# A pad of 160 bytes behind a small table, and where the tiles behind it lie

## The chip, the cores and the metric

One core of a Trainium2 chip runs the whole kernel in one launch. The metric is the device time of one execution in microseconds, given as the median of several runs. A measurement of a change against this kernel can tell about 0.2%, some 3 us, from no change.

## The reference, cut to what matters

One encoder layer on 256 tokens of 2048 features, in float32:

```python
proj = rms_norm(x, attn_norm) @ w_in            # columns: qa ka va qb kb vb ga gb
ya = windowed_gqa(qa, ka, va, ...)              # 8 query heads, 1024 wide
yb = dilated_attention(qb, kb, vb, ...)         # merged over 3 groups, 512 wide
merged = sigmoid(ga) * (ya @ w_branch_a) + sigmoid(gb) * (yb @ w_branch_b)
x = x + merged @ w_out
hf = rms_norm(x, ffn_norm)
g = dwconv_centred(hf @ w_ffn_gate, conv_w, conv_b)      # 5632 wide
x = x + (gelu(g) * (hf @ w_ffn_up)) @ w_ffn_down
x = x + sigmoid(rms_norm(x, ple_norm) @ w_ple_gate) * (p @ w_ple_proj)
return rms_norm(x, final_norm)
```

Nearly all of the work is in the products with weight matrices; the weights are read once, 277 MB in all.

## The kernel before, in words

**Pairs.** A float32 number is kept as two parts, a high one and a low one, both in the fast matmul type. A weight block is 128 x 128. Weights come from memory in pieces of 16 blocks (`raw`, line 174); ACT rounds a run of 8 blocks to `whi` (line 190), DVE subtracts to get `wlo` (line 191). An activation tile holds for each block of 128 features 512 columns: 256 tokens' high parts and 256 low parts, 2048 bytes per partition. `block` (lines 195 to 206) issues two matmuls for each weight block, here called a pair: line 201 holds `whi` and streams all 512 columns, line 202 holds `wlo` and streams the 256 high columns. The held tile is the stationary operand, the streamed one the moving operand. Each matmul has a weight load of its own, which overlaps the matmul before it.

**Moving operands.** `product` (line 207) runs the pairs of one 128-wide slice of outputs, 16 of them for an input of 2048. The streamed tile is given by `movers` (line 662): `hs`, `merged`, `hf`, all named `mov` and taken from the pool `big`; `yab` (line 337), the outputs of the two mixers, 8 and 4 blocks; and `act` (line 682), the gelu half, 22 blocks. `wide_product` (line 214) works the other way round: it holds a slice of the activations and streams the weights, three matmuls for each (lines 224 to 226); the value projections and the last stage use it.

**Order.** `_plan` (line 62) lists the products. First queries, keys and values; then a round for each of 16 slices: the gates `ga` and `gb` (16 pairs each) and, two rounds later, the branch products `ba` (8 pairs from `yab`) and `bb` (4 pairs from `yab`); then the output projection `o`; then for each half of the MLP gate and up products by turns (16 pairs each, 44 products) and 16 down products `d0` or `d1` (22 pairs each from `act`); then the embedding products. The loop at line 672 issues them in this order, and TensorE runs them in order. Attention's small matmuls are put between pairs at fixed places by `run_due` (line 330): scores (lines 430 to 432 and 449), transposes (line 484), values (lines 430 to 432 and 499). The row norms come in the same way: sums (line 285), then a spread over the partitions (line 308), whose moving operand is `rdg` (line 300). In `d1`, `flip` (line 633) puts four transposes after every second product.

**Places in on-chip memory.** Pools are laid one behind the other in the order in which they are opened: constants, `wpool` (`raw`, `whi`, `wlo`), `big` (`mov`), `sc` (small tiles, `tot` first and `tb` behind it), then `att` (`yab`, attention's tiles), whose place `ff` (`act` and the MLP's tiles) takes later. A tile's size is rounded up to 32 bytes per partition. In the built program `raw`, `whi`, `wlo` and every `mov` start at residue 160 modulo 512 bytes; so does `tb`. `tb` takes 80 bytes, rounded to 96. `yab` and `act` both start at 154112, residue 0.

Of the kernel before, what the change touches and what calls it, by code (L numbers as in the profile page):

```python
# [10 lines left out]
F32 = mybir.dt.float32  # L11
# [16 lines left out]
NH = QH + BH  # L28
NBUCK = 32
# [104 lines left out]
def _encoder(ctx: ExitStack, tc, xt, pt, cols, table, onehot, mask, ident_in, last_gain, wts, out):  # L134
# [110 lines left out]
    sc = ctx.enter_context(tc.tile_pool(name="sc", bufs=2))  # L245
# [95 lines left out]
    hba = hb[:, :QH * AW].rearrange("p (h c) -> p h c", c=AW)  # L341
    hbb = hb[:, QH * AW:].rearrange("p (h c) -> p h c", c=BW)
    oh = ap_.tile([NBUCK, 2 * T], F32, name="oh", tag="near", bufs=1)
    tb = sc.tile([NBUCK, NH], F32, name="tb", bufs=1)
    mk = ap_.tile([NH, 2 * T], F32, name="mk", tag="s1", bufs=2)

    order = [(0, 1), (0, 0, 1), (0, 1, 3), (0, 3, 7), (1, 2), (0, 7, 11), (0, 11, PIECE), (2, 3)]
# [440 lines left out]
```

## Time and profile before

| | |
|---|---|
| median of three runs | 1501.67 us (1501.54 to 1502.61) |
| the profiled execution, its own time | 1501.95 us |
| its span | 1500.1 us |
| TensorE busy | 99% of the span |
| VectorE, ScalarE busy | 70%, 51% |
| memory read | 277 MB, 186 GB/s over the span |
| granted TensorE clock | 0.998 |

The span runs from the first to the last instruction that the profiler shows; the time of the execution has 1.85 us around it. A line of the profile names the source line, the engine, the operation, the tile written and the tiles read, in the order moving, then stationary for a matmul. Matmuls overlap: the record of one runs on after the next has begun, so durations do not add up to the time. The time from one start to the next does.

### The profile page before, as it was taken

How to read it: one execution, taken by the hardware profiler on the slowest of the kernel's cores; microseconds unless marked ns; L12 is line 12 of the kernel's file. 1: busy time of each engine (PE TensorE's matmuls, PEld its weight loads, DVE VectorE, ACT ScalarE, POOL GpSimd, SP SyncE). 2: the span in 40 equal slices, each digit the busy share in tenths (PEclk: the TensorE clock that was granted, in tenths of full speed). 3: DMA queues.
4: the chain of work that ended last, by engine and by line, in shares of the span. 5: the costliest groups of instructions: out<-in, count | busy, mean ns of one | idle time of the engine just before them, and what ended most of it. 6: DMA issues, size and time to landing. Idle time of an engine off the chain costs nothing.

```text
span 1500.1 us, 21525 instructions
## 1 busy us (share of the span) xinstructions
PE 1483.0 (99%) x8392; PEld 1292.5 (86%) x8392; DVE 1045.0 (70%) x1631; ACT 767.0 (51%) x1175; POOL 4.6 (0%) x9
## 2 busy tenths in 40 slices
PE   9999999999999999999999999999999999999996
PEld 8888888888888888888888888888888888888885
DVE  7685764666676776778888885557888887656564
ACT  7564544445555555555555554444555555555553
POOL 0000000000000000000000000000000000000000
PEclk9999999999999999999999999999999999999999
DMA  8744344445555555555555555554555555554552
GB/s 316 254 156 182 137 168 172 169 169 188 181 193 196 182 184 204 177 216 194 182 188 194 196 184 183 195 190 180 192 197 191 182 190 196 177 189 172 193 196 84
DMA packets 45233, 280.92 MB, mean 187 GB/s; under 512 B 4996, under 2 KB 9860, under 8 KB 12876
## 3 DMA queue, kind: packets, MB, share of 16 engines
q1 hardware_dynamic: 44268, 277.31, 51.7%
q10 hardware_dynamic: 864, 2.24, 0.4%
q8 instruction: 66, 1.08, 0.3%
q14 instruction: 35, 0.29, 0.1%
HBM read 277.39 MB, written 2.14 MB: 186 GB/s over the span
## 4 chain that ended last, share of the span: by engine, by line
PE 96%; DVE 2%; DMA 1%; ACT 1%; issue 0%; POOL 0%; SPq 0%; DVEq 0%; POOLq 0%; ACTq 0%
PE acc L201 53%; PE acc L202 27%; PE acc L224 4%; PE acc L226 4%; PE acc L225 4%; PE first L201 1%; PE first L202 1%; DVE wlo L191 1%; DMA raw<-in_wts 1%; PE pt L484 0%; PE misc L633 0%; DMA x<-in_xt 0%; PE misc L499 0%; PE sp L449 0%; ACT whi L190 0%
## 5 line engine op out<-in xcount | busy, mean ns | idle before, releaser
L191 DVE TENSOR_TENSOR wlo<-raw,whi 128x1024 fp32r<-128x1024 f32 (+1 forms) x519 | 632.0, 1218 | 407.4 <-ACT whi L190 407.1
L201 PE MATMUL acc<-mov,whi 128*128 128x512 f32 x2608 | 911.4, 394 | 1.5 <-DVE v L539 1.5
L190 ACT ACTIVATE whi<-raw 128x1024 fp32r<-128x1024 f32 (+1 forms) x519 | 547.6, 1055 | 645.0 <-PE acc L201 394.0
L202 PE MATMUL acc<-mov,wlo 128*128 128x256 f32 x2608 | 728.2, 279 | 0.0
L201 PEld LDWEIGHTS acc<-mov,whi 128*128 128x128 f32 x2608 | 488.6, 187 | 112.0 <-DVE v L539 1.7
L202 PEld LDWEIGHTS acc<-mov,wlo 128*128 128x128 f32 x2608 | 491.9, 189 | 0.2
L201 PE MATMUL acc<-act,whi 128*128 128x512 f32 x704 | 247.5, 394 | 0.0
L202 PE MATMUL acc<-act,wlo 128*128 128x256 f32 x704 | 196.5, 279 | 0.0
L201 PEld LDWEIGHTS acc<-act,whi 128*128 128x128 f32 x704 | 131.9, 187 | 31.1
L202 PEld LDWEIGHTS acc<-act,wlo 128*128 128x128 f32 x704 | 132.0, 187 | 0.0
L224 PE MATMUL acc<-whi,mov 128*128 128x512 f32 (+1 forms) x256 | 96.9, 379 | 0.0
L226 PE MATMUL acc<-whi,mov 128*128 128x512 f32 (+1 forms) x256 | 96.6, 377 | 0.0
L225 PE MATMUL acc<-wlo,mov 128*128 128x512 f32 (+1 forms) x256 | 96.6, 377 | 0.0
L252 ACT ACTIVATE t<-acc 128x256 f32<-128x256 f32 x227 | 83.1, 370 | 23.2 <-PE acc L202 23.2
L256 DVE TENSOR_TENSOR u<-acc,t 128x256 f32<-128x256 f32 x196 | 81.3, 418 | 2.4 <-ACT t L252 2.4
L201 PE MATMUL acc<-yab,whi 128*128 128x512 f32 x192 | 68.4, 395 | 0.0
L224 PEld LDWEIGHTS acc<-whi,mov 128*128 128x128 f32 x256 | 48.6, 190 | 9.3 <-DVE wlo L191 0.8
L226 PEld LDWEIGHTS acc<-whi,mov 128*128 128x128 f32 x256 | 48.6, 190 | 8.8
L225 PEld LDWEIGHTS acc<-wlo,mov 128*128 128x128 f32 x256 | 48.6, 190 | 8.6
L202 PE MATMUL acc<-yab,wlo 128*128 128x256 f32 x192 | 53.8, 280 | 0.0
L201 PEld LDWEIGHTS acc<-yab,whi 128*128 128x128 f32 x192 | 36.0, 188 | 8.8
L201 PE MATMUL first<-mov,whi 128*128 128x512 f32 x112 | 39.0, 400 | 0.8 <-DVE mov L269 0.8
(137 smaller groups left out, 856.5 us busy)
## 6 DMA issues: line engine op xcount, KB each, us to landing
raw<-in_wts SPq DMA_DIRECT2D x251, 1024.0 KB, 4.8
raw<-in_wts SPq DMA_DIRECT2D x12, 512.0 KB, 6.9
x<-in_xt SPq DMA_DIRECT2D x13, 128.0 KB, 6.0
mov<-hold SPq DMA_DIRECT2D x3, 514.0 KB, 6.4
mov<-hold SPq DMA_DIRECT2D x2, 768.0 KB, 7.1
mov<-in_last_gain ACTq DMA_DIRECT2D x1, 1024.0 KB, 4.8
out<-mov SPq DMA_DIRECT2D x2, 384.0 KB, 2.5
out<-mov ACTq DMA_DIRECT2D x2, 384.0 KB
```

The lines of the kernel that those rows point to most:

```text
L190: nc.scalar.activation(hi, src, AF.Copy)
L191: nc.vector.tensor_tensor(lo, src, hi.bitcast(F32), op=ALU.subtract)
L201: nc.tensor.matmul(acc, hi[:, o, :], m, start=first, stop=False, skip_group_check=True)
L202: nc.tensor.matmul(acc[:, T:], lo[:, o, :], m[:, :T], start=False, stop=last, skip_group_check=True)
L224: nc.tensor.matmul(acc, xh, hi, start=(k == 0), stop=False)
L225: nc.tensor.matmul(acc, xh, lo, start=False, stop=False)
L226: nc.tensor.matmul(acc, xl, hi, start=False, stop=(k == n - 1))
L252: keep(nc.scalar.activation(t, acc[:, T:], AF.Copy, scale=scale))
L256: nc.vector.tensor_tensor(u, acc[:, :T], t, op=ALU.add)
```

## The change

The table tile gets 40 more columns, which nothing writes or reads; the kernel uses the first 20 as before.

```diff
     oh = ap_.tile([NBUCK, 2 * T], F32, name="oh", tag="near", bufs=1)
-    tb = sc.tile([NBUCK, NH], F32, name="tb", bufs=1)
+    tb = sc.tile([NBUCK, NH + 40], F32, name="tb", bufs=1)[:, :NH]
     mk = ap_.tile([NH, 2 * T], F32, name="mk", tag="s1", bufs=2)
```

`tb` then takes 240 bytes, rounded to 256, so every tile behind it moves up by 160 bytes: the rest of `sc`, `yab` and `act` (to 154272, residue 160), and all of attention's and the MLP's tiles. The tiles ahead of it stay. On every engine the instructions and their order are the same in both programs.

## The prediction

> **What bounds the kernel now.** I read the page first (shares, chain), then a table of stretches that holds only the L201 matmuls, then the timeline where a stretch begins.
>
> ```profile
> span 1500.1 us, 21525 instructions
> PE 1483.0 (99%) x8392; PEld 1292.5 (86%) x8392; DVE 1045.0 (70%) x1631; ACT 767.0 (51%) x1175; POOL 4.6 (0%) x9
> PE 96%; DVE 2%; DMA 1%; ACT 1%; issue 0%; POOL 0%; SPq 0%; DVEq 0%; POOLq 0%; ACTq 0%
> ```
>
> TensorE is busy 99% of the span and holds 96% of the chain that ended last. Nothing else can be late enough to matter, so this change is worth what it does to the time from one matmul to the next. The page's duration of a matmul does not show that: matmuls overlap in the records.
>
> ```profile
> L201 PE MATMUL acc<-mov,whi 128*128 128x512 f32 x2608 | 911.4, 394 | 1.5 <-DVE v L539 1.5
> L201 PE MATMUL acc<-act,whi 128*128 128x512 f32 x704 | 247.5, 394 | 0.0
> L201 PE MATMUL acc<-yab,whi 128*128 128x512 f32 x192 | 68.4, 395 | 0.0
> ```
>
> By these rows mov, act and yab cost the same (394, 394, 395 ns). So I take the pitch instead: the length of a stretch in which TensorE never idles, divided by the pairs (one L201 and one L202 matmul) that start in it. The view: stretch in us from the span's start, its length, busy time of the L201 matmuls, and their count, which takes in one or two that run over an edge.
>
> ```profile
> 169.52:177.65 8.13, 8.13 (x25) 1.00 0.31 123
> 191.27:214.50 23.23, 23.23 (x68) 1.00 0.51 182
> 288.63:311.86 23.23, 23.23 (x69) 1.00 0.49 181
> 326.06:346.91 20.85, 20.85 (x61) 1.00 0.53 184
> 346.91:559.02 212.11, 212.11 (x610) 1.00 0.53 189
> 351.47:362.22 10.75, 10.75 (x33) 1.00 0.53 193
> 565.17:649.62 84.45, 84.45 (x239) 1.00 0.54 190
> 661.70:894.66 232.96, 232.96 (x674) 1.00 0.54 192
> 894.66:1017.86 123.20, 123.20 (x353) 1.00 0.53 189
> 1017.86:1261.93 244.07, 244.07 (x706) 1.00 0.53 190
> 1261.93:1388.67 126.74, 124.25 (x353) 1.00 0.50 183
> ```
>
> There are three beats, all at a granted clock of 1.00. **Middle:** the first half's down products (894.66 on), 16 products of 22 blocks, 352 pairs: 123.20/352 = 350.0 ns. Their moving operand is act. **Fast:** the gate and up products (661.70 on), 42 products of 16, 672 pairs: 232.96/672 = 346.7 ns; the second half's, 704 pairs: 244.07/704 = 346.7. **Slow:** the output projection (565.17 on), 239 pairs: 84.45/239 = 353.3; the first gate products of the mixers (326.06 on), 59 pairs: 20.85/59 = 353.4. Fast and slow stretches read the same kind of tile, mov, with the same two shapes. In the addresses that the built program gives its tiles, raw, whi, wlo and all mov tiles lie at residue 160 modulo 512 bytes, and yab and act at 0; each block is a multiple of 512 bytes, so the residue holds for every block.
>
> So residue 0 gives one beat, 350.0, and residue 160 gives two, 3.3 ns either side of it. Which one holds is not set by address: it is kept until something interrupts the stream, for 672 pairs in one row and 239 in the other. What starts each beat can be read too:
>
> ```profile
> 169.07 0.50 PE L201 MATMUL acc<-mov,whi 128*128 128x512 f32 x1 [1.52 <-DVE v L539]
> 564.23 0.87 PE L201 MATMUL acc<-mov,whi 128*128 128x512 f32 x2
> 658.84 0.59 PE L308 MATMUL misc<-rdg,ones 128*128 128x256 f32 x2
> 324.81 1.06 PE L499 MATMUL misc<-far,vf 128*128 128x128 f32 x8
> 64.87:66.95 2.08, 2.08 (x7) 1.00 0.99 377
> 659.62:661.70 2.08, 2.08 (x8) 1.00 0.47 110
> ```
>
> A stream that resumes from a wait is slow: after 169.07 (23 pairs in 8.13 us, 353.5) and after 564.23, where the second matmul starts late. After the spread of the row norms (L308) it was fast both times (the last two rows: six pairs in 2.08 us, 346.7). After a far head's last small matmuls (L499) it was fast twice (67 pairs in 23.23 us from 191.27 and from 288.63) and slow in the last case, from 326.06. And when the stream comes back from yab it is fast: from 351.47, 31 pairs in 10.75 us, 346.8; the whole mixers' row, 608 pairs at 348.9, says that the other rounds are alike. The residue 0 of yab thus resets the beat for the mixers today, and act resets it for the second half.
>
> **The change part by part.** It makes tb 160 bytes longer per partition. No instruction is added, removed or moved on any engine, and no wait; the DMA into tb writes the same 20 columns. Every tile allocated behind tb moves up by 160 bytes; x, raw, whi, wlo, mov and tot, in front of it, stay. yab and act come to residue 160, so all L201/L202 pairs are then of the kind with two beats. The sum is made against the profiled execution's 1501.95 us (span 1500.1 and 1.85 around it), 0.28 above the median of 1501.67.
>
> Step 1, first half's down products: 352 pairs from 350.0 to 346.7, -1.2 us. If slow, +1.2.
>
> Step 2, second half's: also 352 pairs, but eight groups of four transposes (L633) interrupt them. If all stay fast, -1.2 us, and the halting pairs after a reset go:
>
> ```profile
> 1262.28 0.39 PE L201 MATMUL acc<-act,whi 128*128 128x512 f32 x1
> 1262.63 0.42 PE L201 MATMUL acc<-act,whi 128*128 128x512 f32 x1
> 1263.02 0.39 PE L201 MATMUL acc<-act,whi 128*128 128x512 f32 x1
> 321.63:323.75 2.12, 2.12 (x8) 1.00 0.58 243
> 77.94:80.37 2.43, 2.43 (x8) 1.00 0.71 297
> 85.36:87.78 2.42, 2.42 (x8) 1.00 0.29 122
> ```
>
> The pair at 1262.63 takes 390 ns, 40 too many, and such a pair comes after some of the transposes too: about -0.2 us. The last three rows say how transposes leave a stream of residue 160: after eight of them slow (six pairs in 2.12 us, 353), after four fast (seven in 2.43 and in 2.42, 347 and 346). The flips are of four, but with other operands, so I take most of the products as fast: -0.8 us, bounds -1.4 and +1.2.
>
> Step 3, the mixers, 346.91 to 559.02: 13 rounds of 44 pairs and 36 at the end, 608 pairs in 212.11 us. All fast would be 608 x 346.7 ns = 210.8, -1.3 us; all slow 608 x 353.3 = 214.8, +2.7. Nothing interrupts them now except yab itself, and that reset goes with the change. So one draw, made at 324.81, decides 667 pairs together with the 59 before, which are slow now: fast there is another -0.4. I take fast: -1.7 us.
>
> Step 4, the output projection: it starts with the wait at 564.23, which stays because the last merged block is late by the same work on ACT and DVE. Slow as now: 0, with -1.6 (239 x 6.7 ns) as the other bound.
>
> Step 5, gate and up products, 1376 pairs from 661.70 on. Their beat is drawn once, at 658.84, and act no longer redraws it at 1017.86. The operands of that interruption stay where they are, except rdg, which moves with the change. Kept fast: 0. Slow: 1376 x 6.7 = +9.2 us.
>
> Step 6, attention's small matmuls (s, qf, kf, near, v): their own time is a few us in all, but they redraw the beat of the pairs between 64 and 326 us. I take 0, bounds -1 and +2. The DVE and ACT operations on moved tiles lie beside a busy TensorE; were that cover gone, they could be late only at the four or five waits already there.
>
> Step 7, the 48 matmuls of the embedding product with pw, which moves from residue 0 to 160 and is held while whi streams:
>
> ```profile
> 1396.11:1398.45 2.34, 2.34 (x12) 1.00 0.00 0
> 1401.74:1437.00 35.26, 35.26 (x157) 1.00 0.52 182
> ```
>
> Ten starts in 2.34 us with pw, 234 ns, against 155 in 35.26 with mov, 227: 48 x 7 ns = -0.3 us.
>
> Sum: -1.2 - 0.8 - 1.7 + 0 + 0 + 0 - 0.3 = -4.0 us; 1501.95 - 4.0 = 1497.95, which I round to **1498.0**.
>
> **The rivals.**
>
> *One slow draw in the mixers.* At 324.81 the stream comes out slow, as it does in the trace of before, and now no yab resets it. Price: +2.7 in place of -1.7, so the sum is -1.2 - 0.8 + 2.7 - 0.3 = +0.4 us, 1502.4. For it: that very draw is slow now, and two of the four alike were. Against it: the operands of L499 move, so the draw is made anew.
>
> *The lock turns against the long stage.* This is the slower side. If the stream leaves the L308 spread at 658.84 slow, then 1376 gate and up pairs and 352 down pairs stay slow up to the flips: +9.2 + 1.2, with the second half's down products near 0 and the mixers at -1.7 or +2.7: 1501.95 + 10.4 - 2.0 = 1510.4 or 1514.8. It decides from about half of these pairs slow. Against it: both spreads of the trace, 595 us apart and with different work ahead of them, ended fast, so that interruption seems to set the beat by itself. For it: rdg, its moving operand, shifts from residue 448 to 96, and slow beats are otherwise as common after interruptions as fast ones.
>
> *The residue is not the cause.* If act and yab run at 350.0 because of their place elsewhere (another distance to the weights, another block count), nothing but draws changes: 1501.7, within a microsecond or two. Against it: yab and act have different block counts (8, 4 and 22) and the same beat. The Trainium skill speaks for this rival: "SBUF — State Buffer", section "Who interferes with whom", gives TensorE two independent SBUF read ports, one for the moving operand and one for the weights, and says that TensorE never waits on anyone; by that rule no address could change a pitch and the time would stay. The 346.7, 350.0 and 353.3 ns above do not look like that.
>
> **How the numbers follow.** Chances: forecast 0.45, slow mixers 0.24, slow long stage 0.23, residue not the cause 0.08. The forecast's own range is 1495.5 to 1500.5 by the bounds of steps 2, 4 and 6; slow mixers 1501 to 1505; slow long stage 1507 to 1517. To hold eight in ten the range has to take in the first two and the near part of the third: 1495.5 to 1510.5. A measurement of this kernel tells about 0.2%, 3 us, from no change, so faster means under 1498.7: most of the forecast, 0.37. Slower means over 1504.7: the long stage and a little of the slow mixers, 0.27. The rest, 0.36, is within.
>
> **What would show it.** In the changed profile the down products should take 346.7 ns a pair over 352 pairs (122.0 us in place of 123.20), and no 390 ns pair should follow their start. The mixers should take 210.8 us from the first a-product to the output projection. The page's durations should stay at 394. The forecast is wrong if act still runs at 350.0, if one of the three long stretches shows 353.3, or if a new wait appears on TensorE.

## The result, and the profile after

The change makes the kernel slower: 1516.56 us in the median of four runs (1510.56 to 1517.9) against 1501.69 (1501.54 to 1502.61), ratio 1.0088 with a 95% interval of 1.0069 to 1.0106. The forecast was 1498.0, with a range from 1495.5 to 1510.5. The profiled execution took 1517.9 us, its span is 1516.1.

From the page of the changed kernel: span, chain by engine, and two groups of L201.

```profile
span 1516.1 us, 21525 instructions
PE 98%; DVE 1%; ACT 0%; DMA 0%; issue 0%; DVEq 0%; POOLq 0%; POOL 0%; ACTq 0%
L201 PE MATMUL acc<-mov,whi 128*128 128x512 f32 x2608 | 925.0, 399 | 1.5 <-DVE v L539 1.5
L201 PE MATMUL acc<-act,whi 128*128 128x512 f32 x704 | 248.9, 398 | 0.0
```

The count of instructions is the same, and TensorE holds the chain as before. No new wait stands in these rows, and yet the mov group has 13.6 us more busy time (925.0 against 911.4). The mean record is longer by 4 or 5 ns in both groups.

The table of stretches of the changed kernel, cut where the stages begin. Columns: stretch, length, busy time of L201 and their count, granted clock, DMA share, GB/s. The rows are attention, mixers, output projection, the first gate product with the row norms, gate and up of the first half, its down products, gate and up of the second half, its down products.

```profile
60.12:349.61 289.49, 189.13 (x529) 1.00 0.47 172
349.61:564.44 214.83, 214.83 (x610) 1.00 0.51 187
564.44:655.08 90.64, 90.57 (x258) 1.00 0.51 188
655.08:667.19 12.11, 11.39 (x33) 1.00 0.61 224
667.19:904.63 237.44, 237.44 (x673) 1.00 0.52 189
904.63:1029.02 124.39, 124.39 (x354) 1.00 0.51 186
1029.02:1277.75 248.73, 248.73 (x705) 1.00 0.51 186
1277.75:1404.66 126.91, 124.45 (x353) 1.00 0.51 182
```

The stages of before that the prediction did not show, attention, projection and row norms:

```profile
58.94:346.91 287.97, 187.48 (x529) 1.00 0.48 173
559.02:649.62 90.60, 90.53 (x257) 1.00 0.53 189
649.62:661.70 12.08, 11.36 (x34) 1.00 0.61 225
```

Divided by their pairs, the long rows of after are all at the slow beat: mixers 214.83/608 = 353.3 ns, gate and up 237.44/672 = 353.3 and 248.73/704 = 353.3, first down products 124.39/352 = 353.4. Not one is at 350.0 any more. The middle beat of residue 0 is gone, as the mechanism said, and what took its place is the wrong one of the two.

| stage | before | after | difference, us |
|---|---|---|---|
| up to attention | 58.94 | 60.12 | +1.18 |
| attention | 287.97 | 289.49 | +1.52 |
| mixers | 212.11 | 214.83 | +2.72 |
| projection, row norms | 102.68 | 102.75 | +0.07 |
| gate and up, both halves | 477.03 | 486.17 | +9.14 |
| down, first half | 123.20 | 124.39 | +1.19 |
| down, second half | 126.74 | 126.91 | +0.17 |
| embedding stage and end | 111.43 | 111.44 | +0.01 |
| span | 1500.1 | 1516.1 | +16.0 |

The beat of the long stage is taken in the timeline of the changed kernel at the spread of the row norms: start, duration, engine, line, tiles.

```profile
664.29 0.59 PE L308 MATMUL misc<-rdg,ones 128*128 128x256 f32 x2
...
665.07 0.40 PE L201 MATMUL acc<-mov,whi 128*128 128x512 f32 x1
...
665.43 0.40 PE L201 MATMUL acc<-mov,whi 128*128 128x512 f32 x1
...
665.78 0.40 PE L201 MATMUL acc<-mov,whi 128*128 128x512 f32 x1
```

The pairs behind L308 start at 665.07, 665.43, 665.78: 360 and 350 ns, the slow pattern. It then holds through the next three rows of the table above, 1728 pairs, and into the second half's down products up to the first flip.

### The profile page after: what moved, and what is told of

It reads as the page before. It is cut to its first block, busy times and chain, and to the rows that moved or that the text cites. A ratio compares the mean times of both kernels' runs of the same rounds, so it can differ in the third digit from the quotient of the medians.

```text
span 1516.1 us, 21525 instructions
## 1 busy us (share of the span) xinstructions
PE 1499.0 (99%) x8392; PEld 1297.5 (86%) x8392; DVE 1045.8 (69%) x1631; ACT 767.1 (51%) x1175; POOL 4.7 (0%) x9
## 4 chain that ended last, share of the span: by engine, by line
PE 98%; DVE 1%; ACT 0%; DMA 0%; issue 0%; DVEq 0%; POOLq 0%; POOL 0%; ACTq 0%
PE acc L201 54%; PE acc L202 27%; PE acc L224 4%; PE acc L226 4%; PE acc L225 4%; PE first L201 2%; PE first L202 1%; PE pt L484 0%; DMA x<-in_xt 0%; PE misc L633 0%; PE misc L499 0%; PE sp L449 0%; PE misc L430 0%; PE sp L430 0%; PE sp L432 0%; PE misc L432 0%
## 5 line engine op out<-in xcount | busy, mean ns | idle before, releaser
L201 PE MATMUL acc<-mov,whi 128*128 128x512 f32 x2608 | 925.0, 399 | 1.5 <-DVE v L539 1.5
L201 PEld LDWEIGHTS acc<-mov,whi 128*128 128x128 f32 x2608 | 490.0, 188 | 122.0 <-DVE v L539 1.7
L201 PE MATMUL acc<-act,whi 128*128 128x512 f32 x704 | 248.9, 398 | 0.0
L201 PEld LDWEIGHTS acc<-act,whi 128*128 128x128 f32 x704 | 132.2, 188 | 32.0
L201 PE MATMUL acc<-yab,whi 128*128 128x512 f32 x192 | 68.5, 399 | 0.0
L201 PEld LDWEIGHTS acc<-yab,whi 128*128 128x128 f32 x192 | 36.1, 188 | 9.0
L201 PE MATMUL first<-mov,whi 128*128 128x512 f32 x112 | 40.3, 409 | 1.2 <-DVE mov L269 1.2
```

The source lines that it names most:

```text
L201: nc.tensor.matmul(acc, hi[:, o, :], m, start=first, stop=False, skip_group_check=True)
```

## The experiments

Theory A is that of the prediction: the distance between the places of the moving and the stationary operand decides which beats there are; equal residues have two, one of them is taken at each interruption and kept, and a tile at residue 0 resets it. (`raw`, `whi` and `wlo` lie at 160 in every program here, so for the pairs a distance and a place of the moving tile alone are not told apart.) The rivals are that the moved small tiles or attention's tiles did it, or that residue 160 in act is bad by itself.

### The pad behind sc: rdg back at its place

```diff
-    yab = ap_.tile([P, QH + HG, 2 * T], FR, name="yab", bufs=1)
+    yab = ap_.tile([P, (QH + HG) * 2 * T + 40], ...)[:, 40:]      # and act in the same way
```

`tb` is as before; yab, act and attention lie where the change put them.

> The 160 bytes sit at the front of yab and of act instead of in tb: yab, act and all tiles behind them are where the change put them, but the small tiles of sc, rdg with them, are back at their old places. Theory A (the two beats of residue 160 are drawn at each interruption, and nothing resets them once yab and act lie at 160 too): the down products are fast or slow, never 350.0 ns; the mixers are one beat all through. If the place of rdg is what turned the L308 spread to the slow beat, the gate and up stage is fast again and the time some 10 us below the changed kernel, near 1506; if only the phase in which the stream reaches the spread decides, it can be slow here too, 1510 to 1517, and the runs differ among themselves. Rival B (act and yab at 160 do nothing, the moved small tiles of sc are the cause): 1501.7 and down products at 350.0.

1505.26 us in the median of ten (1498.9 to 1506.91), ratio 1.0015 (1.0002 to 1.0028). Mixers, first gate and up, first down:

```profile
349.03:563.86 214.83, 214.83 (x609) 1.00 0.53 187
666.59:899.54 232.95, 232.95 (x673) 1.00 0.54 192
899.54:1021.57 122.03, 122.03 (x353) 1.00 0.54 190
```

The long stage is fast, and now the down products run at 122.03/352 = 346.7 ns: the gain of step 1, in full. The mixers are slow as in the changed kernel. Of the ten times two are at 1498.9 and eight at 1505 to 1507; the two groups are further apart than the mixers alone can make (4.1 us), and the faster one was not profiled. One and the same program thus comes out in two groups of times; that the beat is what differs between them is not shown.

### Only rdg moved

```diff
-        dg = sc.tile([P, T], F32, name="rdg", bufs=1)
+        dg = sc.tile([P, T + 128], F32, name="rdg", bufs=1)[:, 40:40 + T]
```

The other tiles behind it move by multiples of 512 bytes, so they keep their residues. `sq` has one buffer in place of two here and in yab_only below, to make room. That alone does nothing to the long stage, which takes 232.96 us in yab_only.

> Everything as before the change but one tile: rdg, the moving operand of the L308 spread, lies at residue 96, as in the changed kernel, in place of 448. (sq gets one buffer in place of two to make room.) Theory A2 (the place of rdg decides with which beat the stream leaves the spread): the first half's gate and up products, 672 pairs, are at 353.3 ns, +4.5 us; yab and act at residue 0 still reset the mixers and the second half, which stay as before; 1505 to 1507. Rival (the slow beat of the changed kernel came with the slow mixers and projection ahead of it, not from rdg): 346.7 ns and 1501.7.

1506.8 us (1505.96 to 1508.0), ratio 1.0030 (1.0018 to 1.0042). Mixers, first gate and up, first down, second gate and up:

```profile
348.37:560.48 212.11, 212.11 (x609) 1.00 0.53 189
663.20:900.63 237.43, 237.43 (x673) 1.00 0.53 188
900.63:1023.84 123.21, 123.21 (x354) 1.00 0.53 188
1023.84:1267.90 244.06, 244.06 (x705) 1.00 0.53 190
```

One tile of 1 KB per partition, read by two small matmuls, turns 672 pairs slow: 237.43/672 = 353.3 ns. Then act at residue 0 takes 350.0, and behind it the stream is fast again. This is both parts of the theory in one table: moving rdg alone turns the beat behind this spread, and residue 0 resets it.

It is not the whole rule. The row norms are spread twice, and in this program rdg lies at 96 both times. The stretches just ahead of and behind the first spread, then the second:

```profile
63.66:65.07 1.41, 1.41 (x5) 1.00 0.82 193
66.21:68.29 2.08, 2.08 (x8) 1.00 1.00 377
657.52:659.95 2.43, 2.43 (x7) 1.00 0.26 105
661.08:663.20 2.12, 2.12 (x8) 1.00 0.47 108
```

The first spread takes a slow stream (four pairs, 352.5 ns) and leaves it fast (six, 346.7); the second takes a fast one (seven, 347) and leaves it slow (six, 353). The changed kernel does the same. In the trace of before, with rdg at 448, the two streams come in slow and fast as well, and both leave fast. So the place of rdg decides together with something else, perhaps the beat that comes in; with one spread of each kind that stays open.

### Only yab, only attention, only act

```diff
-    yab = ap_.tile([P, QH + HG, 2 * T], FR, name="yab", bufs=1)
+    yab = ap_.tile([P, (QH + HG) * 2 * T + 128], ...)[:, 40:40 + ...]   # yab_only: rest at its residue
+    yab = ap_.tile([P, (QH + HG) * 2 * T + 40], ...)[:, :...]           # attention_only: the rest 160 further
+    held["act"] = ff.tile([P, FHALF * 2 * T + 40], ...)[:, 40:]         # act_only
```

> Everything as before but yab, which lies at residue 160. (sq with one buffer.) Theory A (yab at 0 resets the beat today, without it the draw of the last values matmuls holds): the mixers are one beat, as drawn at 324.8 us, which before was slow: 353.3 ns a pair, 214.8 us in place of 212.1, total about 1504.4; if that draw comes out fast, 210.8 and 1500.4. The long stage as before, 346.7 and 350.0. Rival (the attention tiles' place made the mixers slow): 212.1 us, 1501.7.

> Everything as before but the tiles of attention behind yab (near, far, s, kf, qf, v and the others), which lie 160 bytes further, as in the changed kernel. Theory A: the stage from 60 to 347 us, 288.0 us before and 289.5 in the changed kernel, is 289 to 290; the mixers are reset by yab and take 212.1; 1503. Rival (the longer stage of the changed kernel came from yab, act or rdg): 288.0, 1501.7.

> Of the change only act is left: yab, attention and sc are as before, act (both halves) and the MLP's small tiles lie 160 bytes further. Theory A: the mixers are as before (reset by yab), the spread ends fast as before, so the first half's down products run at 346.7 ns and the gate and up products of both halves stay at 346.7; the second half's are mixed after the flips. Time 1499.0 to 1501.0. Rival B (the residue of act does nothing): 1501.7 and 350.0 ns. Rival C (residue 160 in act is bad by itself, always slow): 353.3 ns in both halves and 353.3 in the second gate and up stage, 1501.7 + 1.2 + 4.7 + 1.2 = 1508.8.

Mixers of yab_only and of attention_only, then attention in attention_only:

```profile
349.50:564.32 214.82, 214.82 (x610) 1.00 0.53 186
348.61:560.72 212.11, 212.11 (x609) 1.00 0.53 189
60.59:348.61 288.02, 187.72 (x529) 1.00 0.49 173
```

In this one run yab alone costs the mixers the whole 2.7 us: without the reset the stream keeps the slow beat with which it comes in. The single time of yab_only, 1507.23, holds something else too: the granted clock was 0.55 for some 3.6 us from 160.5 on in that run, which by that share is some 1.6 us (an estimate) and makes its attention stage 289.67 us long. Attention's tiles alone do nothing to the mixers, and the expected +1.5 us of the attention stage did not come either (288.02 against 287.97; one run, 1503.62). So that term is not explained by the place of these tiles alone. The sum hides changes both ways, though: the matmuls of the stretch from 257.54 take 20.03 us in place of 19.67, and the 59 pairs ahead of the mixers turn fast, 20.46 us in place of 20.85.

pad_behind_sc, in which yab lies at 160 as well, has the whole term. Its attention stage, then two stretches of the changed kernel that the prediction showed as fast, 67 pairs in 23.23 us:

```profile
59.31:349.03 289.72, 189.34 (x528) 1.00 0.48 172
192.72:216.39 23.67, 23.67 (x68) 1.00 0.48 178
290.88:314.55 23.67, 23.67 (x68) 1.00 0.47 178
```

Behind these two far heads the stream is slow now, 353.3 ns, in pad_behind_sc too, which makes 0.9 of the 1.5 us. Up to the mixers TensorE reads and writes the same addresses in attention_only and in pad_behind_sc, and yet these stretches are fast in the first (23.23 us from 193.25) and slow in the second (23.67 from 192.15). So the places that TensorE uses do not settle the beat alone; what else does is open.

act_only took 1501.17 us in the median of ten, ratio 0.9997 (0.9987 to 1.0006), no difference. Its first down products, second gate and up, and second down products:

```profile
896.02:1018.05 122.03, 122.03 (x354) 1.00 0.53 190
1018.05:1262.10 244.05, 244.05 (x706) 1.00 0.54 190
1262.10:1389.39 127.29, 124.90 (x353) 1.00 0.52 183
```

Residue 160 is not bad by itself: the first half gains 1.2 us. The second half loses 0.55: its pairs are fast up to the first flip and slow behind every flip, 353.3 ns (the 41 pairs from 1281.27 take 14.47 us); in the mean, without the interrupted ones, 352.3 ns.

### The map over residues

In these four act is moved, to another place in each half, and the MLP's small tiles behind it with it; the weights stay at 160. Each is one run: 1505.78, 1500.04, 1504.85 and 1502.91 us in the order of the expectations.

```diff
+            skip = (16 if n == 0 else 32)      # 64 and 128; then 48 and 64, 80 and 96, 56 and 24
+            held["act"] = ff.tile([P, FHALF * 2 * T + 32], ...)[:, skip:skip + FHALF * 2 * T]
```

> As before the change, but act of the first half lies at residue 64 and of the second at 128, to map the pitch over residues (weights at 160). Theory A: each residue has its own beat or beats, between 346.7 and 353.3 ns, and a lone beat wherever the distance to the weights is not small; 1501 to 1504. Rival B: 350.0 in both halves, 1501.7.

> The same with residues 192 for the first half and 256 for the second: 32 and 96 bytes beyond the weights instead of short of them. Theory A: as above, and if the sign of the distance matters these differ from 128 and 64. Rival B: 350.0 in both halves, 1501.7.

> As before the change, with act of the first half at residue 320 and of the second at 384, 160 and 224 bytes beyond the weights. Theory A: one lone beat each, like 0 and 256, no two beats; 346.7 to 350.0 ns, 1500 to 1503. Rival B: 350.0.

> As before the change, with act of the first half at residue 224 (64 bytes beyond the weights) and of the second at 96 (64 short of them). Theory A: 224 fast alone like 192, or already the middle beat like 256; 96 with a slow beat among its beats, since 64 and 128 showed one. Rival B: 350.0 in both.

For each kernel, in the order of the expectations, the down products of the first half, the gate and up products behind them and, for the first two, the down products of the second half:

```profile
895.04:1017.07 122.03, 122.03 (x353) 1.00 0.54 190
1017.07:1265.81 248.74, 248.74 (x706) 1.00 0.53 186
1265.81:1392.55 126.74, 124.36 (x353) 1.00 0.51 183
```

```profile
893.92:1015.95 122.03, 122.03 (x353) 1.00 0.54 191
1015.95:1260.01 244.06, 244.06 (x705) 1.00 0.54 190
1260.01:1386.74 126.73, 124.26 (x353) 1.00 0.52 183
```

```profile
893.78:1015.82 122.04, 122.04 (x354) 1.00 0.54 190
1015.82:1264.55 248.73, 248.73 (x706) 1.00 0.53 186
```

```profile
895.14:1017.95 122.81, 122.81 (x353) 1.00 0.54 189
1017.95:1262.01 244.06, 244.06 (x706) 1.00 0.54 190
```

| act at, weights at 160 | pair in the first half | the 704 pairs behind it |
|---|---|---|
| 0 (before) | 350.0 ns | fast, 346.7 |
| 64 and 320 | 346.7 | slow, 353.3 |
| 160, coming in fast | 346.7 | fast |
| 160, coming in slow | 353.4 | slow |
| 192 | 346.7 | fast |
| 224 | 348.9 | fast |

64 and 320 do the same. In the second half, cut up by the flips, 0 and 256 take the same time (126.74 and 126.73 us). That alone says little, since 128 takes 126.74 too, but the starts agree as well: at 256 the third pair takes 390 ns, as it does at 0, while at 128 it takes 360. 128 and 384 share a pattern of their own, pairs of 361 and 346 ns by turns (353.5 in the mean), with fast stretches of 346.7 behind some flips; 96 runs at 353.3. In these pairs a shift of 256 bytes changes nothing: what counts here is the place modulo 256, not 512. The rival that the residue does nothing has fallen, and so has my expectation that a larger distance gives a lone beat and nothing more: at 64 and 320 the matmuls themselves are fast, but they hand the stream on slow, and both times came out above their forecasts. 224 is neither of the two beats expected for it. 192, 32 bytes beyond the weights, was the candidate: fast, and left fast.

### Every moving operand at 192

`sq` has one buffer here to make room.

```diff
+    gap = big.tile([P, 8], F32, name="gap", bufs=1)      # mov to 192; yab and act by 40 columns, too
```

> A version that could beat both: every moving operand (mov, yab, act) lies 32 bytes beyond the residue of the weights, at 192 with the weights at 160, after act at 192 ran at 346.7 ns. If 192 has the fast beat alone, whatever comes before, then all pairs take 346.7 ns, the projection too (239 pairs, -1.6 us), the down products (-2.4), the start and attention (some 160 pairs, -1.1) and the mixers (-1.3): about 1495 to 1497. If 192 only kept the fast beat that it was given, the beat is drawn at each interruption as at 160, and the time is anywhere from 1496 to 1516. The products that stream weights (L224 to L226) change their distance too, by a sign: 226.7 ns a matmul if that does nothing.

1497.71 us (1497.05 to 1499.25), ratio 0.9973 (0.9962 to 0.9983). Attention, mixers, projection, the first half's gate and up, the second half's down products, then the embedding stage with all of its matmuls:

```profile
59.80:347.32 287.52, 186.74 (x529) 1.00 0.49 173
347.32:558.09 210.77, 210.77 (x609) 1.00 0.54 190
558.09:647.09 89.00, 88.93 (x258) 1.00 0.54 192
...
659.07:892.03 232.96, 232.96 (x673) 1.00 0.54 192
...
1258.11:1383.61 125.50, 122.94 (x353) 1.00 0.53 184
1383.61:1485.29 101.68, 101.68 (x441) 1.00 0.41 149
```

Every long row is at the fast beat: the mixers at 210.77/608 = 346.7 ns, the projection too, although it still begins with a wait. So 32 bytes beyond the weights only the fast beat is seen in a long row here, behind a wait, the spreads, the far heads and the flips. rdg lies at 480 in this program and at 448 in the next; the place that turned the stream slow in rdg_only, 96, was not tried with it. The last row pays for the change: 101.68 us, where before took 99.20 for the same work.

### And the held activations of the last stage back at 160

`sq` and `es` have one buffer here to make room.

```diff
+    def moving(skip):
+        t = big.tile([P, KC * 2 * T + 128], FR, name="mov")
+        return t[:, skip:skip + KC * 2 * T].rearrange("p (k c) -> p k c", c=2 * T)
-            held["pl"] = big.tile([P, KC, 2 * T], FR, name="mov")
+            held["pl"] = moving(0)                        # hs, merged, hf: moving(8); yab, act at 192
```

> The version with residue 192 for the streamed activations, without its loss in the last stage: hs, merged, hf, yab and act at 192, but pl, which the last stage holds while it streams the weights, back at 160. Theory A (what counts is how far the moving operand lies beyond the stationary one; 32 bytes beyond is always fast, 32 short is 233.5 ns in place of 226.7 for a 512-wide matmul): the last stage falls back from 101.7 us to 99.2, all pairs stay at 346.7, and the time is 2.4 us below mov_192, near 1495.3. Rival (the last stage was longer for another reason, the shifted small tiles): 1497.7.

1496.17 us (1494.94 to 1496.36), ratio 0.9960 (0.9945 to 0.9974): the fastest version here. Its median is 1.5 us below that of mov_192, where 2.4 was expected. The embedding stage of before, then of this version:

```profile
1388.67:1487.87 99.20, 99.20 (x441) 1.00 0.44 153
1382.05:1481.25 99.20, 99.20 (x441) 1.00 0.42 153
```

The stage is back at 99.20 us to the hundredth. There the weights stream and the activations are held, so activations 32 bytes further along mean weights 32 bytes short of them. There that costs time, 233 ns a matmul in place of 226.7, and in the pairs 32 bytes short (act at 128) ran partly slow, where 32 beyond ran fast. The sign matters.

### The changed kernel once more

> The changed kernel once more, for how its times spread and for a second profile. Theory A: each execution draws the beat of the mixers and of the long stage anew, so the profile shows stages at 346.7 or 353.3 ns whole, and the times fall in groups: about 1516 with both slow, 1512 with the mixers fast, 1506 with the long stage fast. Rival (the slow beat comes with the addresses, always): one group at 1516 to 1518.

1517.17 us (1515.15 to 1518.42), ratio 1.0099 (1.0084 to 1.0114), and the second profile has the stages of the first to 0.01 us (289.49, 214.83, 90.64, 237.44, 124.38, 248.74). One group, not several: for the changed kernel the draw is nearly always the same. The theory's picture of a fresh draw in each execution was wrong here; only the 1510.56 of the first four runs stands apart. It lies some 6 us below the others, as the two fast times of pad_behind_sc do. Attention's 1.5 us and the 667 pairs from 324.8 us on at 6.7 ns (4.5 us), all fast, would make such a gap (an estimate); no such execution was profiled, so that is not shown.

## Why the prediction was wrong

The mechanism held in the main: two beats at residue 160, one in the middle at residue 0, kept until interrupted. What failed is which beat is taken.

**Step 5 failed**, and it is the bulk: I took the 1376 gate and up pairs as fast, 0 us, because both spreads in the trace of before ended fast, and read from it that "that interruption seems to set the beat by itself". It was +9.14. rdg_only shows that moving its moving operand is enough to turn the beat, though the first spread, with rdg at 96 too, still ends fast. The step had named rdg as the one operand of that interruption that moves, and still treated two outcomes with rdg in its old place as evidence for the new one.

**Step 3 failed** too: -1.7 forecast, +2.72 measured, the price of the slow rival to 0.02 us. The draw at 324.81, slow in the trace of before, was taken as fast with no row that favoured it, and came out slow again. yab_only shows that the missing reset is enough.

**Step 1** had the right size and the wrong sign, +1.19 for -1.2, and follows from step 5: the stream comes in slow. With rdg in its old place it is -1.17. **Step 2**: +0.17 for -0.8, within its bounds by luck: the groups of four transposes, read as leaving the stream fast, left it slow behind four of the seven flips that pairs follow, and in act_only behind all seven. **Step 4**: 0.04 for 0, right. **Step 6**: +1.52 for 0, within its bounds; it is redrawn beats, as the step allowed, but what set them stays open, since attention_only did not show it and pad_behind_sc did. (The small matmuls' own time is not "a few us" but some 32 us from start to start in the trace of before; it enters no sum.) **Step 7**: no gain for -0.3; the ten starts with pw went from 2.34 to 2.30 us, 230 ns and not 227, and the whole stage did not get shorter. The slow start of 1.18 us need not be part of the change: in the experiments in which TensorE reads the same places up to there, attention begins anywhere from 57.99 to 60.59 us.

The slower rival, with the mixers slow too, was worked out at 1514.8; that with attention's 1.5 and the start's 1.2 is the 1517.9 of the profile, 0.4 us apart. I gave the whole rival 0.23, and cut the range through it. It deserved more: it hung on one draw that the change touches, and the trace held no sample of that draw with rdg moved. The forecast that the page's durations would stay at 394 ns was wrong too; the slow beat shows there as 399.

The Trainium skill's "SBUF — State Buffer", section "Who interferes with whom", by which the two read ports of TensorE are independent, would have given no change. These runs do not agree: 346.7 to 353.4 ns a pair by the operands' places, and 1516.56 against 1496.17 us for kernels with the same matmuls. Whether it is at these ports that the two operands meet is not shown.

## What to carry to other kernels

When TensorE is the bound and every wait is hidden, divide long stretches by their matmuls: a pitch that differs between stages with the same shapes is time that no busy share shows. Where it depends on what came before, place the operands so that only one outcome is seen (here the moving operand 32 bytes beyond the stationary one), instead of betting on the better of two. And a padded tile moves everything behind it, so look at the small tiles too.

## What the runs showed of the hardware

- The pitch of a pair of matmuls depends on the place of the moving operand modulo 256 bytes, with the weights always at 160: 346.7, 348.9, 350.0 or 353.3 ns with the same shapes and clock, 2% between the ends. That a distance from the weights is what counts is likely and was not tried by moving the weights of the pairs.
- At equal residues two pitches are stable, 346.7 and 353.3 ns. The slow one held for 1728 pairs without a break.
- At 32 bytes beyond, the fast one alone was seen in long rows, also behind a wait.
- Which one is taken at equal residues depends on things as small as the place of a 1 KB operand of two matmuls, and not on that alone: the same place left one spread fast and the other slow. By what mechanism in the chip was not tried.
